# Two transformer blocks on one core: router on the unscaled activation, expert tiles in other blocks, split parts in shared places

## The chip, the cores and the metric

The kernel runs on one core of a Trainium2 chip. The metric is the device time of one execution in microseconds (us). All data is float32, and all weights come from HBM in every execution (590 MB). The engines are TensorE (PE), VectorE (DVE), ScalarE (ACT), GpSimd (POOL) and SyncE (SP), which issues most of the transfers.

## The reference, cut to what matters

There are 256 tokens of width 1024. The first block mixes (retention and attention, products with `w_in`, `w_ret_o`, `w_att_o`, `w_o`), then routes each token to 4 of 32 experts. The second block is two layers with a gated mixer or attention, a cross-attention into 256 memory rows, and feed-forward products.

```python
x = x + gt_a * (merged @ w_o)
h = rms_norm(x, g_ffn) * (1 + sc_f) + sh_f       # modulated by a vector computed from c
logits = h @ w_router + b_router                 # 256 x 32
top_val, top_idx = top_k(logits, 4); gates = softmax(top_val)
# for each expert e, over the tokens that chose it:
u = h @ w1[e] + b1[e]                            # 1024 x 2048
a = clamped_swiglu(u[:, ::2], u[:, 1::2])
x += gt_f * gate * (a @ w2[e] + b2[e])           # 1024 x 1024
```

## The kernel before

The work falls into three stages. **Stage one** (to about 350 us of the profiled span) computes the first block up to `w_o`. Its weights arrive in 1 MB tiles in six "raw" places; each half tile is split on ACT and DVE into a high and a low part (`split_now`, L196 and L197) in six places each, and PE multiplies three times (`gemm_nat`, L364). The last two such products are `wo0` and `wo1`; their epilogue (L842 to L847) updates `x`, sums its squares and writes `h2 = x * s2`, where `s2` is the scale row held in `late["ss"]`.

**Stage two** routes and runs the experts in 16 pairs, with 64 slots for each expert. The order of the jobs is `c0, c1, h0, c2, h1, ..., c15, h14, h15`: `chunk(p)` multiplies the gathered tokens of pair p by `w1` (L1028 on `bank_a`), and `second(p)` multiplies by `w2` (L1028 on `bank_b`), then scatters back (L1096) and adds to `x`. `gather(p, d)` picks the tokens by products with one-hot rows (L997); it is called for pair p + 1 while pair p is multiplied, and for pair 0 all four calls come ahead of the first product.

The expert weights come as double tiles of 2 MB ("big") in eight places, six of which lie where stage one had its raw tiles and split parts, and the first four tiles of pair 0's last step as 1 MB singles in four places of the pool `pa`: tags `x1`, `x2` (loaded first) and `reth`, `retl` (loaded last). SP issues every load in program order, and each waits until its place is free. The last twelve 1 MB tiles (the end of `h14` and all of `h15`) come in six raw places, made new where the big places were.

Before the change the router does this after `wo1`: `rsqrt` of the mean square of a token block, `h2 = h2 * rs + shift` (L897), transposes to `h2T` (L900), logits with 32 experts as rows (L909), bias on ACT (L910), a transpose back (L914), then for each block of 128 tokens the largest eight (L916), their indices, a one-hot and a count (L921); products that number the slots (L923 to L925), the gate weights, an overflow test, and the one-hot rows for pair 0 (L991).

**Stage three** is the second block, again with split weights. Ahead of it `mem_t` transposes and splits the memory rows after `h15` (L559), `mem_k(0)` multiplies them (L398 to L400), and the normed `x` is transposed (L1197) for the next product with `a_w_in` (L364).

Of the kernel before, what the change touches and what calls it, by code (L numbers as in the profile page):

```python
# [18 lines left out]
P = 128  # L19
# [77 lines left out]
class Weights:  # L97


    def __init__(self, tc, raw, nraw):  # L100
# [3 lines left out]
        self.ahead = 0  # L104
# [6 lines left out]
        self.bigs, self.doubles = None, set()  # L111
# [38 lines left out]
    def load_next(self):  # L150

        i = self.loaded
        if i in self.doubles:
# [3 lines left out]
            t = pool.tile([P, 4096], F32, name="big", tag=tag)  # L157
            v = t.rearrange("p (n k f) -> p n k f", n=2, f=ap.shape[3])
            self.history["big"].append(i)
# [10 lines left out]
    def load_free(self):  # L170

        while self.loaded < (self.limit or len(self.plan)):
            i = self.loaded
            if i not in self.early:
                h, size, n = (self.history["big"], 2, len(self.bigs)) if i in self.doubles else \
                    (self.history["raw"], 1, self.nraw)
                if len(h) >= n and h[-n] + size > self.taken:
                    break
# [11 lines left out]
    def split_now(self, i, half):  # L190
# [3 lines left out]
        hi = self.parts.tile([P, 1024], F32R, name="whi")[:, :k * f].rearrange("p (k f) -> p k f", f=f)  # L194
        lo = self.parts.tile([P, 1024], F32R, name="wlo")[:, :k * f].rearrange("p (k f) -> p k f", f=f)
# [36 lines left out]
def body(tc, A, out, offs, dbg):  # L232
# [6 lines left out]
    parts = ew.enter_context(tc.tile_pool(name="parts", bufs=6, side="right"))  # L239
# [72 lines left out]
    for kind, p_ in jobs:  # L312
        for k in range(0, 8, 2 if kind == "c" else 4):
            for e in (2 * p_, 2 * p_ + 1):
# [41 lines left out]

    def gemm_nat(key, xh, xl, w=512, kt=8, last=False):
# [5 lines left out]
        def mm(tb, xx, wpart):  # L363
            PE.matmul(pss[tb][:, :w], xx, wpart, start=n[tb] == 0, stop=n[tb] == tot - 1)  # L364
# [254 lines left out]
    def ada_late_step(j):  # L619
        if j == 4:  # L620
            late["gta"] = pt.tile([P, D], F32, name="gta")
        if j == 6:
            late["ss"] = pa.tile([P, 2, D], F32, name="ss", tag="reth")
        ada_bcast(j, gtf if j >= 10 else late["gta"] if j < 6 else late["ss"][:, j // 2 - 3])
        if j >= 8 and j < 10:
            hs = slice(j % 2 * 512, j % 2 * 512 + 512)
            g = pt.tile([P, 512], F32, name="gff", tag="aqT" if j == 8 else "akT")
# [93 lines left out]
    pt = ea.enter_context(tc.tile_pool(name="pt", bufs=1, reuse_waits="tile"))  # L721
    M = {}
# [16 lines left out]
    def att_group(g, hp):  # L739
# [6 lines left out]
        qT = pt.tile([P, 2, T], F32, name="aqT", bufs=1)  # L746
        kT = pt.tile([P, 2, T], F32, name="akT", bufs=1)
# [22 lines left out]
    def att_softmax(hp):  # L770
        for a in range(2):
# [3 lines left out]
            for g in range(3):  # L775
# [4 lines left out]
                eT = pt.tile([P, 384], F32, name="eT", bufs=2)  # L780
# [8 lines left out]
    def gate(n, h):  # L789
# [5 lines left out]
        return s_  # L795

    for st_ in stage:
# [27 lines left out]
        elif n[:2] == "wo":  # L825
            h = int(n[2])
            if h == 0:
                for k0 in range(0, 8, 2):
                    b = transpose_to(m1, "b", k0)
                    split(hh[:, k0:k0 + 2], hl[:, k0:k0 + 2], b)  # L830
                rt = pt.tile([P, 1536], F32, name="rt", tag="avt")
# [7 lines left out]
            with tc.high_priority():  # L839
                for tb in range(2):  # L840
# [3 lines left out]
                    late["sq", h] = S.activation(t, xt, AF.Square, accum_out=ss2[:, tb, h:h + 1])  # L844
                    late["h2", h] = V.tensor_tensor(h2[:, tb, hs], xt, late["ss"][:, 1, hs], OP.mult)
                    if h == 0:
                        V.tensor_scalar(ss2[:, tb, :1], ss2[:, tb, :1], 1.0 / D, RMS_EPS, OP.mult, OP.add)  # L847
    dump("x2", x)


    rt_used = [4]
# [4 lines left out]
    W.bigs = [(upper, f"big{i}") for i in range(6)]  # L856
    W.doubles = {first_b + i for i in range(0, 372, 2) if not 12 <= i < 16}
# [6 lines left out]
    def small(p, *shape):  # L864
        n = int(np.prod(shape))
        v = rt[:p, rt_used[0]:rt_used[0] + n]
        rt_used[0] += n
        if len(shape) == 2:
            v = v.rearrange("p (a b) -> p a b", a=shape[0])
        if len(shape) == 3:  # L870
# [703 lines left out]
```

## Time and profile before

| what | value |
|---|---|
| median of 3 runs | 1929.1 us (1927.86 to 1931.21) |
| the profiled execution's own time | 1928.28 us |
| its span, first to last instruction | 1926.6 us |
| PE busy | 1841.6 us (96%) |
| DVE, ACT busy | 803.5 us, 536.6 us |
| mean granted TensorE clock | 0.984 |
| read from HBM | 590.37 MB, 307 GB/s over the span |

PE is busy for most of the span in all three stages, but its busy time is modelled and does not say who waits for whom. The transfers run at 427 GB/s in most of stage two and at 145 to 300 GB/s in stage three.

### The profile page before, as it was taken

The page shows a single profiled execution, that of the slowest core. Times are in us where ns is not written, and L with a number is a line of the kernel's source. Part 1 is how long each engine was busy: PE and PEld are TensorE (multiplying, and loading weights), DVE is VectorE, ACT ScalarE, POOL GpSimd, SP SyncE. Part 2 cuts the span into 40 slices and gives each one's busy share as a digit, 9 for nine tenths or more (in the row PEclk, how much of TensorE's full clock was granted, in tenths as well). Part 3 has the DMA queues.
Part 4 walks back from the last instruction along what each step waited for, and adds up shares of the span by engine and source line. Part 5 has one row for each costly group of instructions (what it writes and reads, how often), then busy time and mean ns, then how long its engine had stood idle before and what let it go on. Part 6 is the DMA issues. An engine that isn't in the chain of part 4 may idle for free. (4 is left out here: it accounts for less than half of the span.)

```text
span 1926.6 us, 23931 instructions
## 1 busy us (share of the span) xinstructions
PE 1841.6 (96%) x10132; PEld 1212.7 (63%) x10132; DVE 803.5 (42%) x1283; ACT 536.6 (28%) x792; POOL 2.6 (0%) x7
## 2 busy tenths in 40 slices
PE   7999999899999999998999899899999999999998
PEld 6899987543344434333333344238889998879997
DVE  5787477422221212221112212028564457565445
ACT  3545454210000000000000000005544445645443
POOL 0000000000000000000000000000000000000000
PEclk9999999999999999999999999999999999999999
DMA  9777476999999999999999999998455555326550
GB/s 359 254 261 249 151 257 229 372 404 416 427 426 427 427 427 427 426 428 427 427 427 427 427 426 427 424 370 294 142 180 190 179 193 176 111 97 225 181 175 23
DMA packets 160403, 593.05 MB, mean 308 GB/s; under 512 B 7643, under 2 KB 92214, under 8 KB 134690
## 3 DMA queue, kind: packets, MB, share of 16 engines
q1 hardware_dynamic: 154008, 583.25, 77.4%
q10 hardware_dynamic: 6282, 8.21, 1.4%
q8 instruction: 81, 1.33, 0.3%
q14 instruction: 32, 0.26, 0.0%
HBM read 590.37 MB, written 1.07 MB: 307 GB/s over the span
## 5 line engine op out<-in xcount | busy, mean ns | idle before, releaser
L1028 PE MATMUL bank_a<-big,hg 128*64 128x512 f32 x2016 | 478.3, 604 | 17.0 <-DMA big<-in_w_mlp 16.9
L197 DVE TENSOR_TENSOR wlo<-raw,whi 128x1024 fp32r<-128x1024 f32 x286 | 345.4, 1222 | 252.7 <-ACT whi L196 251.7
L196 ACT ACTIVATE whi<-raw 128x1024 fp32r<-128x1024 f32 x286 | 298.2, 1058 | 346.9 <-issue 101.0
L1028 PEld LDWEIGHTS bank_a<-big,hg 128*64 128x64 f32 x2016 | 146.5, 139 | 304.1 <-issue 269.4
L1028 PE MATMUL bank_b<-big,apk 128*64 128x512 f32 x928 | 223.6, 617 | 20.7 <-DMA big<-in_w_mlp 20.7
L400 PE MATMUL bank_b<-xh,wlo 128*128 128x256 f32 x640 | 181.1, 283 | 0.0
L398 PE MATMUL bank_b<-xh,whi 128*128 128x256 f32 x640 | 181.1, 283 | 0.0
L399 PE MATMUL bank_b<-xl,whi 128*128 128x256 f32 x640 | 181.0, 283 | 0.0
L1028 PEld LDWEIGHTS bank_b<-big,apk 128*64 128x64 f32 x928 | 84.1, 141 | 148.5 <-issue 93.4
L1050 DVE COPY us<-bank_a 128x512 f32<-128x512 f32 x32 | 22.1, 692 | 345.9 <-PE bank_a L1028 345.9
L398 PEld LDWEIGHTS bank_b<-xh,whi 128*128 128x128 f32 x640 | 122.7, 192 | 0.7
L399 PEld LDWEIGHTS bank_b<-xl,whi 128*128 128x128 f32 x640 | 122.6, 192 | 0.7
L400 PEld LDWEIGHTS bank_b<-xh,wlo 128*128 128x128 f32 x640 | 122.7, 192 | 0.0
L352 ACT ACTIVATE us<-bank_a 128x512 f32<-128x512 f32 x32 | 19.1, 597 | 328.9 <-PE bank_a L1028 328.9
L1086 DVE TENSOR_TENSOR y<-bank_b,gtf 128x512 f32<-128x512 f32 x32 | 22.1, 692 | 201.6 <-PE bank_b L1028 200.1
L352 ACT ACTIVATE spread<-bank_b 128x256 f32<-128x256 f32 x16 | 6.1, 384 | 299.2 <-PE bank_b L1096 299.2
L997 PEld LDWEIGHTS bank_b<-ohg,h2c 128*128 128x128 f32 x512 | 66.1, 203 | 23.0 <-issue 21.1
L997 PE MATMUL bank_b<-ohg,h2c 128*128 128x128 f32 x512 | 72.7, 294 | 0.0
L1499 PE MATMUL bank_a<-wlo,ah 128*128 128x512 f32 x176 | 69.8, 396 | 0.0
L1500 PE MATMUL bank_a<-whi,al 128*128 128x512 f32 x176 | 69.7, 396 | 0.0
L1498 PE MATMUL bank_a<-whi,ah 128*128 128x512 f32 x176 | 69.7, 396 | 0.0
L352 ACT ACTIVATE hg<-bank_b 128x256 f32<-128x256 f32 x64 | 24.6, 384 | 149.2 <-PE bank_b L997 149.2
(382 smaller groups left out, 2735.2 us busy)
## 6 DMA issues: line engine op xcount, KB each, us to landing
big<-in_w_mlp SPq DMA_DIRECT2D x184, 2048.0 KB, 27.0
raw<-in_w_ffn_in SPq DMA_DIRECT2D x44, 1024.0 KB, 5.1
raw<-in_w_in SPq DMA_DIRECT2D x38, 1024.0 KB, 7.5
raw<-in_w_ada SPq DMA_DIRECT2D x24, 1024.0 KB, 6.6
raw<-in_w_ffn_out SPq DMA_DIRECT2D x22, 1024.0 KB, 4.9
raw<-in_w_mlp SPq DMA_DIRECT2D x16, 1024.0 KB, 14.7
raw<-in_b_w_in SPq DMA_DIRECT2D x10, 1024.0 KB, 5.2
raw<-in_w_mix_out SPq DMA_DIRECT2D x8, 1024.0 KB, 5.2
```

The lines of the kernel that those rows point to most:

```text
L196: self.nc.scalar.activation(hi, w, AF.Copy)
L197: self.nc.vector.tensor_tensor(lo, w, hi.bitcast(F32), OP.subtract)
L352: return S.activation(o, i, AF.Copy, **kw)
L398: PE.matmul(v[:, m], hi[:, k, ms], xh[:, k], start=k == 0, stop=False)
L399: PE.matmul(v[:, m], hi[:, k, ms], xl[:, k], start=False, stop=False)
L400: PE.matmul(v[:, m], lo[:, k, ms], xh[:, k], start=False, stop=k == 7)
L997: PE.matmul(b[:, n], h2c[:, tb, c0:c0 + 255:2], ohs[p_][:, tb], start=tb == 0, stop=tb == 1)
L1028: last[:] = [PE.matmul(out[at], st, w, start=start, stop=stop)]
L1050: V.tensor_copy(us[:, c + 1], u[c + 1])
L1498: PE.matmul(ops[tb, h], ah[:, k, ts], hi[:, k, hs], start=n + k == 0, stop=False)
L1499: PE.matmul(ops[tb, h], ah[:, k, ts], lo[:, k, hs], start=False, stop=False)
L1500: PE.matmul(ops[tb, h], al[:, k, ts], hi[:, k, hs], start=False, stop=n + k == 11)
```

## The change

- The router multiplies the unscaled `h2` (no `rsqrt`, no shift), with tokens as rows. The scale `rs` is applied to the logits on DVE together with a bias row `br`, to which shift times `w_router` has been added earlier (16 small transposes of the shift row to columns `shc` and 8 products, at the start of `wo0`). The transposes are placed behind the last product of `wo1`.
- `h2c` is `h2 * rs` without the shift; the shift is added when a gather leaves PSUM: on ACT for pair 0, on DVE for the others.
- The one-hot rows of pair 0 come directly behind the slot numbers; the gate weights follow, and the overflow test, the transposed gates and `spread_pair(0)` follow chunk 0.
- Of pair 0 only the first gather comes ahead of the products; the other three are called within chunk 0. The transposes of the expert bias (`b1T`) come ahead of that gather, behind the logits, and the loads of the bias rows go from SP's queue to POOL's.
- A new 16 KB place `mid` in `pa` holds the attention's small tiles, then the first double tile and every eighth later, then small tiles of stage three. It replaces the big place `middle`. The four singles now go to `reth`, `retl`, `x2`, `x1` in this order, with the first double ahead of the third; `late["ss"]` moves from `reth` to `x1`.
- A high and a low part share one of six places, taken in turn.
- The double at 370 becomes two single loads (`lone`), in the last big places; the memory rows become a planned 1 MB load ahead of `h15`'s tiles, and `mem_t` moves ahead of `h15`. The load of `g_final` goes to POOL's queue.

```diff
         pss = [bank("a") for _ in range(2)]
...
-            PE.matmul(pss[tb][:, :w], xx, wpart, start=n[tb] == 0, stop=n[tb] == tot - 1)
+            latest[:] = [PE.matmul(pss[tb][:, :w], xx, wpart, start=n[tb] == 0, stop=n[tb] == tot - 1)]
...
-        hi = self.parts.tile([P, 1024], F32R, name="whi")[:, :k * f].rearrange("p (k f) -> p k f", f=f)
-        lo = self.parts.tile([P, 1024], F32R, name="wlo")[:, :k * f].rearrange("p (k f) -> p k f", f=f)
+        both = self.parts.tile([P, 2, 1024], F32R, name="whl", tag=f"whl{(self.splits + self.shift) % 6}")
+        self.splits += 1
+        hi, lo = [both[:, n, :k * f].rearrange("p (k f) -> p k f", f=f) for n in range(2)]
...
             if h == 0:
+                for k in range(8):
+                    PE.transpose(b[:, k:k + 1], late["ss"][:1, 0, k * P:(k + 1) * P], ident[:1, :1])
+                    d0 = k // 2 * 256 + k % 2
+                    PE.transpose(b[:, 8 + k:9 + k], late["ss"][:1, 0, d0:d0 + 255:2], ident[:1, :1])
+                copy_s(shc.rearrange("p a k -> p (a k)"), b[:, :16])
+                b = bank("b")
+                for k in range(8):
+                    PE.matmul(b[:, :32], shc[:, 0, k:k + 1].to_broadcast([P, P]), wr[:, k], start=k == 0, stop=k == 7)
+                V.tensor_tensor(br, br, b[:, :32], OP.add)
...
-    W.bigs = [(upper, f"big{i}") for i in range(6)]
...
-    W.load_early(first_b + 12, pa.tile([P, 2048], F32, name="raw", tag="x1"))
-    W.load_early(first_b + 13, pa.tile([P, 2048], F32, name="raw", tag="x2"))
-    for _ in range(6):
+    W.bigs = [(pa, "mid")] + [(upper, f"big{i}") for i in range(6)]
...
+    W.lone = {first_b + 370, first_b + 371}
...
+    W.load_early(first_b + 12, pa.tile([P, 2048], F32, name="raw", tag="reth"))
+    W.load_early(first_b + 13, pa.tile([P, 2048], F32, name="raw", tag="retl"))
+    W.load_next()
+    W.load_early(first_b + 14, pa.tile([P, 2048], F32, name="raw", tag="x2"))
+    for _ in range(5):
...
-            scaled = V.scalar_tensor_tensor(h2[:, tb, hs], h2[:, tb, hs], rs, late["ss"][:, 0, hs], OP.mult, OP.add)
...
+        with after(latest[0]):
+            for tb, h in ((0, 0), (0, 1), (1, 0), (1, 1)):
+                b = bank("a" if tb > h else "b").rearrange("p (k t) -> p k t", k=4)
+                for k in range(4):
+                    PE.transpose(b[:, k], h2[:, tb, (4 * h + k) * P:(4 * h + k + 1) * P], ident)
...
+                for k in range(4 * h, 4 * h + 4):
+                    dotted = PE.matmul(lt[:, tb * 32:tb * 32 + 32], h2T[:, k, tss[tb]], wr[:, k], start=k == 0, stop=k == 7)
+        for tb in range(2):
+            if tb:
+                with after(picked):
+                    rs.append(rsqrt(ss2[:, 1, 1:], 1.0 / D, ss2[:, 1, :1], 1))
+            V.scalar_tensor_tensor(lg[:, tb], lt[:, tb * 32:tb * 32 + 32], rs[tb], br, OP.mult, OP.add)
...
+        routed = V.tensor_tensor(ohs[0], con("slots")[:, None, None, :SLOTS].to_broadcast([P, 2, 2, SLOTS]),
+                                 R[:, :, :2, None].to_broadcast([P, 2, 2, SLOTS]), OP.is_equal)
+        with after(copied):
+            for tb in range(2):
+                copy_s(h2c[:, tb], h2[:, tb], scale=rs[tb])
...
-    nc.sync.dma_start(b2, A["b_mlp2"][0])
+    nc.gpsimd.dma_start(b2, A["b_mlp2"][0])
...
-        copy_s(hg[:, p_ % 2, :, d0:d0 + 2], b.rearrange("p d e s -> p e d s"))
+        if p_ == 0:
+            for n in range(2):
+                S.activation(hg[:, 0, :, d0 + n], b[:, n], AF.Identity, bias=shc[:, 1, d0 + n:d0 + n + 1])
+            return
+        V.tensor_tensor(hg[:, p_ % 2, :, d0:d0 + 2].rearrange("p e d s -> p d e s"), b,
+                        shc[:, 1, d0:d0 + 2, None, None].to_broadcast([P, 2, 2, SLOTS]), OP.add)
...
+            if p_ == 0 and k < 6:
+                gather(0, k + 2)
...
         if (kind, p_) == ("h", 14):
             W.load_free()
-            mem_load()
-            nc.sync.dma_start(gfin, A["g_final"][None, :].to_broadcast([P, D]))
+            nc.gpsimd.dma_start(gfin, A["g_final"][None, :].to_broadcast([P, D]))
+            mem_t()
```

## Rows read from the trace of the kernel before

**Rows 1.** Busy time, clock, DMA in short stretches and in stage two.
```profile
core 0: us, PE busy (x) PEld busy (x) DVE busy (x) ACT busy (x) POOL busy (x), PEclk, DMA share, GB/s
315.00:325.00 10.00, 10.00 (x44) 7.94 (x43) 5.01 (x5) 4.87 (x6) 0.00 (x0) 1.00 0.02 7
325.00:330.00 5.00, 4.18 (x27) 3.40 (x26) 4.99 (x8) 2.22 (x4) 0.00 (x0) 1.00 0.68 223
365.00:370.00 5.00, 5.00 (x29) 4.88 (x28) 0.00 (x0) 1.16 (x3) 0.00 (x0) 0.58 1.02 434
410.00:420.00 10.00, 10.00 (x51) 4.44 (x51) 2.51 (x6) 0.77 (x2) 0.00 (x0) 1.00 0.85 329
480.00:1150.00 670.00, 635.03 (x2890) 258.41 (x2888) 136.79 (x242) 48.94 (x93) 0.00 (x0) 0.98 1.01 427
...
1282.00:1286.00 4.00, 4.00 (x18) 1.29 (x16) 0.00 (x0) 0.00 (x0) 0.00 (x0) 0.75 0.54 197
```

**Rows 2.** Issues on SP in order of time: start, length, what, how many.
```profile
306.35 19.32 SPq L133 DMA_DIRECT2D raw<-in_w_mlp  x2
...
390.82 0.80 SPq L133 DMA_DIRECT2D big<-in_w_mlp  x2
...
414.20 1.17 SPq L133 DMA_DIRECT2D big<-in_w_mlp  x2
```

**Rows 3.** What SP waited for, 250 to 480 us: total, times, longest.
```profile
SPq L133 <- PE bank_a L1028: 81.9, 9, 22.5
```

**Rows 4.** Instructions in order of time, end of `wo1` to first expert product.
```profile
349.60 0.39 PE L364 MATMUL bank_a<-whi,hl 128*128 128x512 f32 x1
...
352.69 0.21 DVE L431 TENSOR_SCALAR rs_z<-rt 128x1 f32<-128x1 f32 x1
...
354.09 1.41 DVE L897 SCALAR_TENSOR_TENSOR h<-h,rs_y,ss 128x512 f32<-128x512 f32 x2
...
359.52 0.20 DVE L916 MAX8 rt<-bank_b 128x8 f32<-128x32 f32 x1 [0.51 <-PE bank_b L914]
...
360.60 0.37 DVE L921 TENSOR_REDUCE rt<-rt 128x32 f32<-128x128 f32 x1
...
363.44 6.60 PE L997 MATMUL bank_b<-ohg,h2c 128*128 128x128 f32 x32
...
369.97 7.52 PE L1028 MATMUL bank_a<-big,hg 128*64 128x512 f32 x34
```

**Rows 5.** PE in order of time, between chunk 0 and chunk 1.
```profile
397.59 1.09 PE L1008 MATMUL bank_b<-cm,b 64*128 64x64 f32 x8
...
398.89 3.93 PE L997 MATMUL bank_b<-ohg,h2c 128*128 128x128 f32 x32
```

**Rows 6.** Groups by line and shape, 284 to 371 us: busy us, mean ns.
```profile
L909 PE MATMUL bank_b<-h2T,rt 128*32 128x128 f32 x32 | 4.1, 275 | 0.2 <-ACT h2T L352 0.2
...
L559 PE MATMUL bank_b<-cm,m 128*128 128x128 f32 x16 | 2.2, 272 | 0.0
```

**Rows 7.** DVE in order of time: last use of the `g_ffn` row.
```profile
316.88 0.69 DVE L630 SCALAR_TENSOR_TENSOR ss<-ss,gff 128x512 f32<-128x512 f32 x1 [0.99 <-ACT ss L352]
```

**Rows 8.** PE in order of time, start of `h15`.
```profile
1276.15 1.07 PE L1028 MATMUL bank_b<-raw,apk 128*64 128x512 f32 x2
...
1280.34 8.78 PE L1028 MATMUL bank_b<-raw,apk 128*64 128x512 f32 x32 [3.12 <-DMA raw<-in_w_mlp]
```

**Rows 9.** PE in order of time, end of stage two to first product of stage three.
```profile
1301.23 1.38 PE L559 MATMUL bank_b<-cm,mem 128*128 128x128 f32 x8
...
1303.74 0.39 PE L399 MATMUL bank_a<-mem_l,whi 128*128 128x256 f32 x1
...
1309.97 1.04 PE L1197 MATMUL bank_b<-cm,x 128*128 128x128 f32 x8
...
1312.07 0.50 PE L364 MATMUL bank_a<-whi,xh 128*128 128x512 f32 x1 [1.06 <-ACT xh L352]
```

**Rows 10.** DMA issues: queue, count, KB each, median us from issue to landing.
```profile
b<-in_b_mlp SPq DMA_DIRECT2D x3, 128.0 KB, 25.6
...
rt<-in_w_router ACTq DMA_DIRECT2D x1, 128.0 KB, 8.0
```

More of the change, by code (lines that the diff above doesn't have):

```diff
@@ L103, in __init__ @@
         self.loaded = self.done = self.taken = 0
-        self.ahead = 0
+        self.ahead = self.splits = self.shift = 0
         self.parts = None
@@ L110, in __init__ @@
         self.limit = None
-        self.bigs, self.doubles = None, set()
+        self.bigs, self.doubles, self.lone = None, set(), set()
         self.history = {"raw": [], "big": []}
@@ L152, in load_next @@
         i = self.loaded
-        if i in self.doubles:
+        if i in self.doubles or i in self.lone:
             ap = self.plan[i][1]
@@ L174, in load_free @@
             if i not in self.early:
[L175 to L177 removed]
+                h, n = (self.history["big"], len(self.bigs)) if i in self.doubles | self.lone else \
+                    (self.history["raw"], self.nraw)
+                if len(h) >= n and h[-n] + (2 if h[-n] in self.doubles else 1) > self.taken:
                     break
@@ L622, in ada_late_step @@
         if j == 6:
-            late["ss"] = pa.tile([P, 2, D], F32, name="ss", tag="reth")
+            late["ss"] = pa.tile([P, 2, D], F32, name="ss", tag="x1")
         ada_bcast(j, gtf if j >= 10 else late["gta"] if j < 6 else late["ss"][:, j // 2 - 3])
@@ L626, in ada_late_step @@
             hs = slice(j % 2 * 512, j % 2 * 512 + 512)
-            g = pt.tile([P, 512], F32, name="gff", tag="aqT" if j == 8 else "akT")
+            g = mid[:, (j - 8) * 512:(j - 7) * 512]
             nc.scalar.dma_start(g, A["g_ffn"][:, hs].to_broadcast([P, 512]))
@@ L721, in body @@
     pt = ea.enter_context(tc.tile_pool(name="pt", bufs=1, reuse_waits="tile"))
+    mid = pa.tile([P, 4096], F32, name="mid", tag="mid")
+    eTs = [mid[:, 1024 + i * 384:1024 + (i + 1) * 384] for i in range(2)]
     M = {}
@@ L883, in body @@
     ixf = small(P, 2, 8)
+    lg = small(P, 2, 32)
     oh = small(P, 2, 4, 32)
     pick = small(P, 2, 32)
+    ohs = {0: keep.tile([P, 2, 2, SLOTS], F32, name="ohg0", tag="GT")}
     ones = con("ones")
[L887 to L910 removed]
@@ new lines, in body @@
+    gates = small(P, 2, 4)
+    with after(routed):
+        V.tensor_tensor(gates, mx[:, :, :4], mx[:, :, :1].to_broadcast([P, 2, 4]), OP.subtract)
+        S.activation(gates, gates, AF.Exp)
+        gl = small(P, 2)
+        V.reduce_sum(gl, gates, AX.X)
+        V.reciprocal(gl, gl)
+        V.tensor_tensor(gates, gates, gl[:, :, None].to_broadcast([P, 2, 4]), OP.mult)
+        for tb in range(2):
+            V.tensor_tensor(oh[:, tb], oh[:, tb], gates[:, tb, :, None].to_broadcast([P, 4, 32]), OP.mult)
+            V.reduce_sum(G[:, tb], oh[:, tb].rearrange("p k e -> p e k"), AX.X)
@@ L1200, in transposed @@
         return v_, s_
-    mem_t()
     kmT, vm = [], []
-    kv = kv_[0]
+    mid = pa.tile([P, 4096], F32, name="kv", tag="mid")
+    kv = mid[:, :2048].rearrange("p (n i b t) -> p n i b t", n=2, i=2, b=2)
     for n, to in enumerate((kmT, vm)):
@@ L1266, in body @@
         nc.gpsimd.memset(q, 0.0)
[L1268 removed]
+    junk = mid[:, 3584:].bitcast(mybir.dt.bfloat16)
     def normalize(dst, src, st, n, gb):
```

214 lines of the change are left out of this document (96 added, 118 removed).

## The prediction

> **What bounds the kernel now.** I read the short stretches first. In stage two the DMA engines are full at 427 GB/s from 480 to 1150 us [rows 1], and PE, 635 of 670 us busy, waits for tiles now and then: that stage lasts as long as its stream of expert tiles. So the question is when the stream gets going and when it ends.
>
> Two holes stand ahead of it. From 315 to 325 us the queues carry 7 GB/s [rows 1]: SP issued a first single tile at 306.35 us, and the second waits in front of everything else until `x2` is free, 19 us later [rows 2]. The other is at 410 to 420 us, with the DMA share at 0.85 [rows 1]. There the list of issues has nothing between 390.82 and 414.20 us [rows 2], and the wait view gives the reason: 22.5 us for PE in chunk 1 [rows 3]. The eight doubles and four singles are full, and the next places come free only when PE has finished the first step of chunk 1. PE has worked without a wait for data since its first expert product at 369.97 us [rows 4]. So the start of the endless part of the stream hangs on PE, and PE's start on the router: 19.97 us from the last product of `wo1` (350.0) to 369.97 [rows 4]. Filling the first hole alone only makes the second longer.
>
> The end: `h15` waits 3.12 us for a tile, and its first 32 instructions then take 8.78 us [rows 8]. Behind it PE does the memory transposes (1301.23), a dense `mem_k(0)` until 1309.97, the transposes of `x`, and the first product at 1312.07 [rows 9]. Stage three is mostly PE-bound, so what is won before 1312 should stay won.
>
> **The change part by part: the router.** L is the end of the last `wo1` product (350.0 before).
> - PE: 16 transposes at 2.2/16 = 0.14 us and 32 logit instructions at 4.1/32 = 0.13 us [rows 6], 6.3 us; the second block's logits are done at L + 6.3, the first block's about L + 4.3. The new logits load 128 columns and stream 32 instead of the reverse; I take them as equal.
> - DVE: bias and scale (estimate 0.25 us, as the 0.21 of a small operation [rows 4]) and the picking chain, 359.52 to 360.97 = 1.45 us [rows 4], for block one end at L + 6.0. The second `rsqrt` is ordered behind it: 352.69 to 354.09 = 1.4 us [rows 4]. The second chain ends at L + 9.1. The scaling of `h2` (1.41 us [rows 4]), the bias and the transpose back are gone; `h2c` on ACT runs beside this.
> - From the end of the picking to the first gather lie 363.44 − 360.97 = 2.5 us [rows 4], of which I take about 1.0 for gate weights and overflow, now later: L + 10.6.
> - The first gather is a quarter of 3.93 us at full clock [rows 5], 1.0, and its two evacuations 0.4: L + 12.0.
> - The other three gathers are only moved: 2.95 us of PE inside chunk 0. The bias transposes (1.09 us [rows 5]) leave it for a time when PE waits anyway. Net, PE stands where it stood at 369.97 at L + 13.9: 6.1 us won.
> - Against it, 16 one-row transposes and 8 products (two instructions each) enter `wo0`, where PE has no slack but 0.82 us in 325 to 330 [rows 1]. 32 instructions at 0.105 to 0.15 us (my estimate around the 0.13 above) are 3.4 to 4.8, less 0.8: I take 2.6. Bounds 0 (they fit into waits earlier) and 4.0.
> - The clock: in 365 to 370 us it was granted at 0.58 on average, after a thin stretch of PE work, and the 32 gather instructions took 6.60 us instead of 3.93 [rows 1, 4, 5]. Now the first products may meet it. The old number contains 2.7 us of it; I charge 1.3 to the new, between 0 and 2.7, because PE is idle for some 4 us, where it was thinly used from 350 to 363.
>
> The Trainium skill (TensorE: Matmul & The Clock Gate, "What's actually happening") says that the slow clock is the default and sustained activity lifts it. By that the new start pays the 2.7 in full, and the forecast below would be 1.4 us later. The rows agree with the rule in kind.
>
> So the router gives 6.1 − 2.6 − 1.3 = 2.2 us; ends −0.6 and 6.1.
>
> **Loads.** Two singles and the first double can now go while `x2` is still read: `reth` and `retl` are free, and `mid` at 316.88 + 0.69 = 317.57 us [rows 7]. That puts one more single and the double, 3.15 MB, at 427 GB/s 7.4 us, into the first hole. By the paragraph above this is worth nothing by itself; it caps the gain at the front at about 7.4 us, above the 2.2. Its cover is the full set of places at 390 us. Parts that come free in turn let doubles issue a few us earlier; same answer. The bias rows on POOL's queue are priced under the rivals.
>
> **Hidden edits.** Adding the shift on DVE costs at most some 0.7 us for each of 60 gathers (the 512-wide `L630` took 0.69 [rows 7]); DVE is busy 137 of 670 us [rows 1], and the gathers run a pair ahead: nothing, or 2.8 us a pair if PE ever waited for the bank. `lone`, `mid` in stage three and shared places move no bytes.
>
> **The end.** `mem_t` ahead of `h15` falls into the 3.12 us wait [rows 8]. If PE works there, the first 32 instructions take 32 × 7.52/34 = 7.1 us [rows 4] rather than 8.78, and the last tiles, whose places they free, are issued so much earlier; the queue is half empty there (0.54 [rows 1]). I take 1.3 us, bounds 0 and 1.7. The memory tile takes a raw place and so lets one expert tile fewer be ahead, but before, the same bytes stood in the same queue: nothing, at worst one tile, 1.05 MB or 2.45 us. Behind `h15`, transposes and their first wait vanish: `mem_k(0)` runs dense from 1303.74 to 1309.97 [rows 9], 6.2 us, and could start at about 1301.3, where the transposes start now. So it ends at 1307.5: I take 2.5 us, bounds 0 (another load is late then) and 3.6 (the norm of `x` is last then; my estimate of its DVE chain).
>
> **Sum.** 2.2 + 1.3 + 2.5 = 6.0 us off the profiled execution's 1928.28 (its span is 1926.6) gives 1922.3. That execution lies 0.8 under the median of 1929.1, so I forecast 1923.1 for the median. About 0.2% (3.9 us) is what a measurement of this kernel can tell from no change.
>
> **Rivals.**
> - *The stream moves by the full 7.4 us.* If the extra work in `wo0` hides and the clock stays up, PE wins 6.1 or more and the earlier loads are used: 7.4 + 3.8 = 11.2, 1917.9. For it: the hole is real [rows 1]. Against it: PE was full around `wo0`.
> - *The router's gain is eaten.* Both charges at their upper ends: 6.1 − 4.0 − 2.7 = −0.6, leaving 3.8 − 0.6 = 3.2: 1925.9. For it: 10.00 of 10 us of PE in 315 to 325 [rows 1].
> - *The memory transposes do not move.* The order on each engine is set by the builder's own timeline, and `h15` is marked urgent; if PE gets the transposes behind it as before, only 2.2 remain: 1926.9.
> - *Slower: the first gather waits for the bias rows.* The transposes of the bias rows stand ahead of it on PE, and everything behind waits with them. On SP's queue the rows landed 25.6 us after issue, a small load on ACT's queue 8.0 us [rows 10]. If their place (tag `y`) comes free only with the router's tiles, as at L + 10 before, 25.6 us would push the gather some 25 us back: 22 lost at the front, 3.8 won at the end, 1947. At 8.0 us it costs about as much as is won. It decides from a landing later than about L + 20. Against it: the place lies over small tiles of the modulation, whose last use is near 317 us [rows 7], so the loads can go in the empty hole. The Trainium skill (DMA: Bandwidth & Descriptors, "Issuing engines are not separate DMA queues") says that loads from any engine share the same DMA engines and interleave, so that POOL's queue would not by itself bring the rows sooner; the 8.0 beside 25.6 us says that standing behind 2 MB tiles in one queue does matter here.
>
> **How the numbers follow.** Forecast 0.46, full 7.4 us 0.13, eaten gain 0.22, transposes that stay 0.09, late bias rows 0.10. Faster by over 0.2%: 0.46 + 0.13 = 0.59; within: 0.22 + 0.09 = 0.31; slower: 0.10. The likeliest case alone spans 1919 to 1925. The range takes in the second to fourth cases with some slack and leaves the late rows out: 1915.5 to 1930.
>
> **What would show it.** Right: `wo1` ends some 2.6 us later, the first expert product comes at L + 12 to L + 14, the issue at 414.20 moves to about 412, and the empty stretch ahead of it grows by some 5 us; the hole at 315 shrinks; memory transposes near 1274, `h15` without a half-clock start, first product of stage three near 1306. Wrong: no empty stretch at 400 to 412 us (then the loads counted), `wo1` ending later than 354, a PE wait for the bias rows, or a time lost in stage three, where a load of parameters that used to be in time is now late.

## The result and the profile after

The changed kernel took 1938.73 us (median of 7 runs, 1935.62 to 1941.83) beside 1927.86 for the kernel before (7 runs, 1925.51 to 1931.21): a ratio of 1.0055, 95% interval 1.0043 to 1.0067. It is slower by some 10.9 us, outside the stated range of 1915.5 to 1930 and on the other side of the forecast of 1923.1. The profiled execution took 1938.29 us, with a span of 1936.6 against 1926.6.

Four points, each the start of an instruction, cut both spans into five stretches, so the differences add up to the span's, but for rounding.

| stretch, us | before | after | predicted | found |
|---|---|---|---|---|
| to the last product of `wo1` | 349.60 | 358.62 | +2.6 | +9.0 |
| from there to the first issue behind the empty stretch of SP | 64.60 | 62.86 | -4.8 | -1.7 |
| from there to the last product of `h15` | 882.9 | 882.5 | -1.3 | -0.4 |
| from there to the first product of stage three | 14.96 | 15.35 | -2.5 | +0.4 |
| from there to the end | 614.5 | 617.3 | 0 | +2.8 |
| sum | | | -6.0 | +10.0 |

The last product of `h15` starts at (before, then after):

```profile
1297.11 0.59 PE L1028 MATMUL bank_b<-raw,apk 128*64 128x512 f32 x1
...
1303.94 0.59 PE L1058 MATMUL bank_b<-raw,apk 128*64 128x512 f32 x1
```

Short stretches of the changed kernel, as [rows 1] of before: times, busy time and number of instructions by engine, granted clock, DMA share, GB/s.

```profile
315.00:325.00 10.00, 10.00 (x41) 7.40 (x41) 6.52 (x8) 4.99 (x6) 1.59 (x3) 1.00 1.04 360
365.00:370.00 5.00, 1.28 (x7) 1.06 (x6) 4.20 (x22) 1.15 (x1) 0.00 (x0) 0.69 1.00 415
370.00:375.00 5.00, 4.94 (x25) 4.76 (x26) 4.07 (x21) 1.43 (x4) 0.00 (x0) 0.50 1.02 434
380.00:385.00 5.00, 5.00 (x25) 1.56 (x22) 0.00 (x0) 0.00 (x0) 0.00 (x0) 1.00 0.01 3
410.00:420.00 10.00, 9.30 (x51) 3.78 (x49) 6.13 (x10) 3.69 (x5) 0.00 (x0) 1.00 0.63 264
480.00:1150.00 670.00, 635.39 (x2914) 255.88 (x2914) 156.62 (x295) 31.63 (x48) 0.00 (x0) 0.99 1.01 427
```

The hole at 315 is filled (360 GB/s instead of 7), and in exchange the queues run dry at 380 to 385 us and more than before at 410 to 420 (share 0.63 instead of 0.85). Between 480 and 1150 nothing differs. The issues behind still wait for PE, up to 18.2 us at a time, so the early loads seem worth nothing, as predicted; no run took them out alone. What SP waited for between 250 and 480 us, and the issues around the empty stretch (start, length, what):

```profile
SPq L133 <- PE bank_a L1058: 86.6, 10, 18.2
...
402.47 0.80 SPq L133 DMA_DIRECT2D big<-in_w_mlp  x2
...
421.48 0.80 SPq L133 DMA_DIRECT2D big<-in_w_mlp  x2
```

The gap that ended at 414.20 [rows 2] ends at 421.48. It did not grow by some 5 us, as the prediction's sign had it: from start to start it is 19.0 us instead of 23.4. It is the queues that stand empty for longer. The router on PE, as [rows 4]:

```profile
358.62 0.40 PE L373 MATMUL bank_a<-whl,hl 128*128 128x512 f32 x1
358.85 0.60 PE L926 MATMUL bank_b<-cm,h 128*128 128x128 f32 x4
...
362.38 2.87 PE L934 MATMUL bank_b<-rt,h2T 128*128 128x32 f32 x24 [0.25 <-ACT h2T L359]
...
371.69 6.24 PE L1023 MATMUL bank_b<-ohg,h2c 128*128 128x128 f32 x30
377.87 7.09 PE L1058 MATMUL bank_a<-big,hg 128*64 128x512 f32 x32
```

L, the end of the last `wo1` product, is 359.0. The first gather comes at L + 12.7 (before 363.44 - 350.0 = 13.4), and 30 gather instructions stand ahead of the first product at L + 18.9, not 8. On DVE, the first block's bias, the second's, and the one-hot rows:

```profile
365.28 0.25 DVE L939 SCALAR_TENSOR_TENSOR rt<-bank_b,rs_y,rt 128x32 f32<-128x32 f32 x1 [2.23 <-PE bank_b L934]
...
368.29 0.25 DVE L939 SCALAR_TENSOR_TENSOR rt<-bank_b,rs_y,rt 128x32 f32<-128x32 f32 x1
...
370.99 0.42 DVE L951 TENSOR_TENSOR ohg<-cm,R 128x256 f32<-128x256 f32 x1
```

The first block's chain waited for the logits of both blocks (L + 6.3, not L + 4.3). Ahead of `wo0`, the new instructions and the products before them on PE:

```profile
325.20 5.79 PE L373 MATMUL bank_a<-whl,att 128*128 128x512 f32 x24
330.91 0.22 PE L859 MATMUL bank_b<-cm,ss 1*128 1x1 f32 x1
...
332.78 1.97 PE L865 MATMUL bank_b<-rt,shc 128*128 128x32 f32 x16 [0.27 <-ACT shc L359]
334.59 1.94 PE L568 MATMUL bank_b<-cm,m 128*128 128x128 f32 x16
```

The shift row takes PE from 330.91 to 334.59, 3.7 us. The first row holds the surprise: 24 products in 5.79 us. The kernel before does the same 24 (first and last shown) in this time:

```profile
319.69 0.39 PE L364 MATMUL bank_a<-whi,att 128*128 128x512 f32 x1
...
324.91 0.39 PE L364 MATMUL bank_a<-whi,att 128*128 128x512 f32 x1
```

From first start to last start, 23 steps, that is 5.22 us, 0.227 a product; after, (5.79 - 0.39)/23 = 0.235. No wait stands in either. The median over all 128x512 products of stage one at the full clock went from 0.227 to 0.234, 3% more. The end of stage two on PE, as [rows 8] and [rows 9]:

```profile
1283.59 1.91 PE L568 MATMUL bank_b<-cm,raw 128*128 128x128 f32 x16
1285.61 7.94 PE L1058 MATMUL bank_b<-raw,apk 128*64 128x512 f32 x34
1296.63 3.65 PE L1058 MATMUL bank_b<-raw,apk 128*64 128x512 f32 x16 [3.09 <-DMA raw<-in_w_mlp]
...
1314.06 0.29 PE L409 MATMUL bank_a<-mem_h,whl 128*128 128x256 f32 x1
1314.19 1.03 PE L1228 MATMUL bank_b<-cm,x 128*128 128x128 f32 x8
1319.29 1.22 PE L373 MATMUL bank_a<-whl,xh 128*128 128x512 f32 x2 [4.07 <-ACT xh L359]
```

The memory transposes moved as meant, and `h15` runs at the full clock behind them (granted 1.00 at 1282 to 1286 us, 7.94 us for 34 instructions). But PE reaches the end of what has landed and waits 3.09 us there, and 0.60 more at 1300.89, where before it waited 3.12 us [rows 8] and

```profile
1290.35 7.35 PE L1028 MATMUL bank_b<-raw,apk 128*64 128x512 f32 x30 [1.23 <-DMA raw<-in_w_mlp]
```

So the transposes did not fill the wait: it stands further on, and the end of `h15` still follows its last tiles. The memory products behind it run dense, but PE then waits 4.07 us for ACT. What ACT and its queue (ACTq) did:

```profile
1312.42 0.39 ACTq L1280 DMA_DIRECT2D ws<-in_a_w_s  x1
1312.85 2.62 ACTq L1282 DMA_DIRECT2D tri<-in_c_tri  x1
1315.51 0.71 ACTq L1284 DMA_DIRECT2D bsr<-in_a_b_s  x1
1316.27 1.06 ACT L201 ACTIVATE whl<-raw 128x1024 fp32r<-128x1024 f32 x1 [2.92 <-issue]
1317.23 0.58 ACT L359 ACTIVATE kv<-bank_a 128x512 f32<-128x512 f32 x1
1317.71 1.05 ACT L201 ACTIVATE whl<-raw 128x1024 fp32r<-128x1024 f32 x1
1318.65 1.08 ACT L359 ACTIVATE xh<-bank_b 128x512 fp32r<-128x512 f32 x2
```

ACT spent 3.7 us on issuing three loads of tables, then did a split, the copy of `kv` and a second split before the copy that PE waited for.

### The profile page after: what moved, and what is told of

It is laid out like the page before. It is cut to its first block, busy times and chain, and to the rows that moved or that the text cites. A ratio compares the mean times of both kernels' runs of the same rounds, so it can differ in the third digit from the quotient of the medians.

```text
span 1936.6 us, 23949 instructions
## 1 busy us (share of the span) xinstructions
PE 1843.4 (95%) x10162; PEld 1210.6 (63%) x10162; DVE 825.7 (43%) x1342; ACT 514.7 (27%) x735; POOL 4.7 (0%) x11
## 5 line engine op out<-in xcount | busy, mean ns | idle before, releaser
L202 DVE TENSOR_TENSOR whl<-raw,whl 128x1024 fp32r<-128x1024 f32 x286 | 345.6, 1222 | 260.1 <-ACT whl L201 258.7
L201 ACT ACTIVATE whl<-raw 128x1024 fp32r<-128x1024 f32 x286 | 298.6, 1058 | 333.0 <-issue 109.8
L409 PE MATMUL bank_b<-xh,whl 128*128 128x256 f32 x640 | 180.9, 283 | 0.0
L408 PE MATMUL bank_b<-xl,whl 128*128 128x256 f32 x640 | 180.3, 282 | 0.0
L407 PE MATMUL bank_b<-xh,whl 128*128 128x256 f32 x640 | 180.1, 281 | 0.0
L407 PEld LDWEIGHTS bank_b<-xh,whl 128*128 128x128 f32 x640 | 120.9, 189 | 0.6
L408 PEld LDWEIGHTS bank_b<-xl,whl 128*128 128x128 f32 x640 | 120.6, 189 | 0.7
L409 PEld LDWEIGHTS bank_b<-xh,whl 128*128 128x128 f32 x640 | 119.9, 187 | 0.0
L373 PE MATMUL bank_a<-whl,hh 128*128 128x512 f32 x288 | 91.2, 399 | 0.0
L1028 DVE TENSOR_TENSOR hg<-bank_b,shc 128x256 f32<-128x256 f32 x60 | 25.4, 424 | 123.9 <-PE bank_b L1023 123.9
L1531 PE MATMUL bank_a<-whl,al 128*128 128x512 f32 x176 | 69.2, 393 | 0.0
L1529 PE MATMUL bank_a<-whl,ah 128*128 128x512 f32 x176 | 68.8, 391 | 0.0
```

The costliest lines, as they stand in the source:

```text
L201: self.nc.scalar.activation(hi, w, AF.Copy)
L202: self.nc.vector.tensor_tensor(lo, w, hi.bitcast(F32), OP.subtract)
L373: latest[:] = [PE.matmul(pss[tb][:, :w], xx, wpart, start=n[tb] == 0, stop=n[tb] == tot - 1)]
L407: PE.matmul(v[:, m], hi[:, k, ms], xh[:, k], start=k == 0, stop=False)
L408: PE.matmul(v[:, m], hi[:, k, ms], xl[:, k], start=False, stop=False)
L409: PE.matmul(v[:, m], lo[:, k, ms], xh[:, k], start=False, stop=k == 7)
```

## The experiments

The kernel before was run beside each group. Its median was 1927.01 with the first four, then 1928.47, 1927.29 and 1928.25, so ratios are compared, not times; 0.0010 of a ratio is 1.9 us. By their intervals, the difference of two runs' ratios is uncertain by 3 to 4 us, so what a single edit is worth is read from the traces where they can tell.

**Where the operands lie.** `shc` (64 bytes a partition) and `nov` (32) are new in the pool `keep`, and everything in `pa` behind it moved by 96 bytes: `hh` from byte 34272 to 34368 of each partition. In the feed-forward part of stage three `ah` moved from 90688 to 105120. The split weights `whi`, `wlo` or `whl` start 480 past a multiple of 512 in both kernels. (The addresses are those the program assigns when it is built; no trace shows them.)

```diff
 # e1_pad: the changed kernel, plus
+    keep.tile([P, 8], F32, name="pad")
 # e2_pad_both: as e1_pad, plus
+        pf.tile([P, 8], F32, name="pad2")
 # e3_before_pad: the kernel before, plus
+    keep.tile([P, 24], F32, name="pad")
 # e8_shift_right: the changed kernel, plus
+    ew.enter_context(tc.tile_pool(name="pad_r", bufs=1, side="right")).tile([P, 8], F32, name="padr")
```

> The changed kernel with 32 unused bytes in the pool ahead of the activations, so that hh, hl, reth and att lie 32 bytes past a multiple of 64 in each partition, as they did before the change; ah and al then lie on a multiple of 64, as before. Theory places (stage one is longer because its 128x512 products start 234 ns apart instead of 227, and that follows from where the activations lie): the spacing in stage one returns to 227 ns, some 600 products give back 4.0 us, those of stage three's other products 0.8, while the 528 products of the feed-forward part go from 229 to 234 ns and lose 1.9: 2.9 us less, 1935.8. Rival order (the shared places mid and whl changed who waits for whom, and the spacing is a by-product of waits): spacing still 234 in stage one, time within 1 us of 1938.7.

> As the run before, and 32 unused bytes more ahead of ah and al, so that they too lie 32 past a multiple of 64. Theory places: 227 ns in stage one and 227 to 230 in the feed-forward part: 4.8 us less than the changed kernel, 1933.9. Rival order: within 1 us of 1938.7.

> The kernel before with 96 unused bytes in the same pool and nothing else: hh on a multiple of 64, ah 32 past one, exactly where the changed kernel has them. Theory places: stage one loses 4.0 us at 234 ns a product, the last product of wo1 ends near 354, other products of stage three lose 0.8, the feed-forward part gains 1.9: 2.9 us more than before, 1930.8. Rival order: spacing stays 227, time within 1 us of 1927.9.

> The changed kernel with 32 unused bytes at the other end, so that in stage one the split weights whl lie on a multiple of 64 as hh does (stage three's are not moved). Which operand sets the pace: if it is where the activations lie, nothing changes (234 ns, 1938.7); if it is that both lie alike, stage one returns to 227 ns and gains 4.0, 1934.7; if the weights must lie 32 past a multiple of 64, stage one gets slower still. Rival order: 234 ns, within 1 us of 1938.7.

Measured: e1_pad 1938.42, ratio 1.0056 (1.0042 to 1.0070); e2_pad_both 1935.49, 1.0049 (1.0035 to 1.0063); e3_before_pad 1930.14, 1.0014 (1.0005 to 1.0023); e8_shift_right 1936.56, 1.0048 (1.0034 to 1.0062). The same 24 products in e3_before_pad, first and last of them on PE:

```profile
324.71 0.40 PE L365 MATMUL bank_a<-whi,att 128*128 128x512 f32 x1
...
330.10 0.39 PE L365 MATMUL bank_a<-whi,att 128*128 128x512 f32 x1
```

5.39 us instead of 5.22: 96 unused bytes alone turn 0.227 into 0.234, in a kernel with no other edit. The rival (order and shared places) falls. My rule of where hh lies falls too: e1_pad puts it back 32 past a multiple of 64, and the group becomes 5.73 us, 0.232, not 0.227. e8_shift_right moves the other operand and gives the same 5.73, on PE in e1_pad and in e8_shift_right:

```profile
321.79 5.73 PE L374 MATMUL bank_a<-whl,att 128*128 128x512 f32 x24
```

```profile
322.34 5.73 PE L374 MATMUL bank_a<-whl,att 128*128 128x512 f32 x24
```

What these two have in common is the distance from the activations to the split weights, 384 modulo 512. In e2_pad_both (1935.49 instead of the expected 1933.9) stage one has the 0.232 of e1_pad, not 0.227, and the feed-forward part, at distance 256, has 0.227. So the theory became one of distance:

```diff
 # e9_place: the changed kernel, plus
+    keep.tile([P, 40], F32, name="pad")
+        pf.tile([P, 40], F32, name="pad2")
 # e10_before_place: the kernel before, plus
+        pf.tile([P, 104], F32, name="pad2")
```

> The changed kernel with 160 unused bytes ahead of the activations and 160 more ahead of ah and al. After the first runs the theory is narrower: what sets the spacing of 128x512 products is the distance from the left operand's address to the split weights' address, taken modulo 512 bytes. Seen so far: 0 gives 227 ns, 256 gives 228, 288 gives 234, 320 gives 229, 384 gives 232 to 235, 416 gives 234 to 236. Here it is 256 in stage one and 0 in the feed-forward part. Theory distance: 227 to 229 ns in both, the end of wo1 some 4 to 5.5 us earlier, the feed-forward part 1.3 shorter, other products of stage three 0.8: 6 to 7 us less than the changed kernel, 1932.2. Rival (the shared places whl themselves cost, not the distance): stage one stays at 232 or more, at most 2 us won, 1936.7.

> The kernel before with 416 unused bytes ahead of ah and al alone, which brings their distance to the split weights from 416 to 0 modulo 512. Theory distance: the 528 products of the feed-forward part go from 234 to 227 ns, 4.0 us less than before, 1923.0; stage one and two unchanged. Rival: the feed-forward part waits for its weights and not for the products: within 1 us of 1927.0.

Measured: e9_place 1935.33, 1.0039 (1.0024 to 1.0054); e10_before_place 1925.27, 0.9985 (0.9977 to 0.9994). The group in e9_place:

```profile
320.15 5.60 PE L374 MATMUL bank_a<-whl,att 128*128 128x512 f32 x24
```

That is 0.227 again, at distance 256. In the feed-forward part PE starts 707 instead of 700 instructions in 1450 to 1550 us in e10_before_place. The kernel before carried this cost itself, and repairing that alone makes it faster by 0.15%, 2.9 of the 4.0 us expected. In e9_place 3.1 us of the 6 to 7 expected came; the intervals exclude neither 6 nor nothing. The traces can tell: e11_combo (below), which has the places of e9_place, and e5_two_banks have the same code and the same slow stretch up to there, and the last `wo1` product starts at 354.77 and 358.92 us, 4.2 us apart. The rival of the shared places falls, since stage one is at 0.227 with them in use.

**The thin work ahead of wo0.** The new instructions left out:

```diff
 # e4_no_rows: the changed kernel; the 16 transposes, copy_s(shc, ...), 8 products and br + ... replaced by
+                V.tensor_copy(shc.rearrange("p a k -> p (a k)"), late["ss"][:, 0, :16])
```

> The changed kernel without the 16 transposes of the shift row and the 8 products with it ahead of wo0; shc is filled by one copy of other numbers on DVE, so the bias of the logits and the shift of the gathered rows are left out of the computation in effect. Theory thin work: PE saves 3.7 us (330.91 to 334.59 in the profile after), and also the stretch at the lower clock level that begins near 328 to 332 us in five of eight profiles with these instructions and in none without them, 3.4 to 6.8 us long, at half speed up to 3.4 us: 3.7 to 6 us less, about 1934. The prediction's price: 2.6 us less, 1936.1. Rival (wo0's first products wait for their split weights anyway): within 1 us of 1938.7.

Measured: 1933.78, 1.0033 (1.0020 to 1.0045), about 4.2 us less than the changed kernel, nearer to the theory than to 2.6, though the intervals don't part the two. In the traces of e16_gathers_behind, which has these instructions, and e4_no_rows, neither with a slow stretch near 50 or 330 us, the last `wo1` product starts at 355.83 and 352.47: the instructions alone cost 3.4 us. Of the 12 profiles taken of kernels with these instructions, 9 have a stretch at the lower clock level that begins at 326 to 333 us, though the changed kernel's own has none; of the 5 taken without the one-row transposes (before, e3_before_pad, e10_before_place, e4_no_rows, e12_combo_dma) none has. (The expectation's "five of eight" should read five of seven.) Windows of e5_two_banks, columns as above:

```profile
325.00:330.00 5.00, 4.73 (x31) 3.77 (x29) 3.85 (x7) 2.30 (x3) 0.00 (x0) 1.00 0.60 203
330.00:335.00 5.00, 5.00 (x25) 5.00 (x25) 1.48 (x3) 0.60 (x1) 0.00 (x0) 0.50 0.97 342
```

The granted clock is 0.50, 1.2 GHz, right behind the one-row transposes. Its price: in the profile of e14_no_lone, which has it, the last product of `wo1` is

```profile
361.81 0.40 PE L373 MATMUL bank_a<-whl,hl 128*128 128x512 f32 x1
```

and in that of the changed kernel it starts at 358.62, with the same code up to there and the same earlier stretch near 50 us: 3.2 us.

**The router.**

```diff
 # e5_two_banks: the changed kernel
-        lt = bank("b")
+        lts = [bank("b"), bank("b")]
 # e16_gathers_behind: the changed kernel; in chunk 0, behind the products of each step
+            if p_ == 0:
+                with after(*last):
+                    if k < 6:
+                        gather(0, k + 2)
+                    gather(1, k)
```

> The changed kernel with the logits of the two token blocks in two banks of PSUM instead of one, so that the first block's bias need not wait for the second block's 16 products. Theory router chain: the first picking chain starts at L + 4.3 instead of L + 6.4 (L: the end of the last wo1 product), everything behind comes 2 us earlier, the first expert product at L + 17, the first issue of the endless stream 2 us earlier: 1936.7. Rival (the chain is not what the start waits for, as the first products still stand behind three gathers at the slow clock): the first product comes earlier but the issue does not, 1938.7.

> The changed kernel with the later gathers of pair 0 and all of pair 1's ordered behind the products of each step of chunk 0, as the change's description has it; in the changed kernel PE got 30 gather instructions ahead of the first product. The prediction's step (the gathers are only moved, PE has to do them ahead of the first release either way): the first product comes at L + 15.5 instead of L + 19.2, but the first release of the endless stream only as much earlier as fewer gathers fall into the slow stretch, 0 to 1.5 us: 1938. Rival (products at once help): 3.7 us less, 1935.

Measured: e5_two_banks 1936.28, 1.0042 (1.0027 to 1.0057); e16_gathers_behind 1938.49, 1.0052 (1.0039 to 1.0066). In e5_two_banks L is 359.3, and on DVE the first bias starts at

```profile
364.12 0.25 DVE L939 SCALAR_TENSOR_TENSOR rt<-bank_b,rs_y,rt 128x32 f32<-128x32 f32 x1
```

L + 4.8 instead of L + 6.3. The first gather then starts at L + 11.3 instead of 12.7, in all three runs with two banks. On SP the issue behind the empty stretch is

```profile
419.63 0.33 SPq L133 DMA_DIRECT2D big<-in_w_mlp  x1
```

at L + 60.3 instead of 62.5, the 2 us that were expected. In e7_tables, with one bank and L at 360.9, it is

```profile
422.06 0.33 SPq L133 DMA_DIRECT2D big<-in_w_mlp  x1
```

So not all of the 2 us is the bank's. The stretch at the lower clock level behind L lasts 6.8 us in e5_two_banks and 10.2 in the changed kernel, and three runs with one bank and a stretch of 6.8 us (e4_no_rows, e6_mem_behind, e7_tables) have the issue at L + 61.1 to 61.3. So some 1 us is shown for the second bank, and 1.2 us goes with the shorter stretch; whether that one follows from the bank is open. In the three runs with two banks it lasts 6.8 us; of the eleven with one bank three have 6.8, seven 10.2 and one 13.7. In e16_gathers_behind L is 356.2, and PE shows

```profile
368.91 2.07 PE L1023 MATMUL bank_b<-ohg,h2c 128*128 128x128 f32 x8
371.50 8.54 PE L1058 MATMUL bank_a<-big,hg 128*64 128x512 f32 x32 [0.52 <-ACT hg L1026]
```

The first product is at L + 15.3, 3.6 us earlier, and the issue at L + 62.4, where it was, with a slow stretch of the same 10.2 us. So it is the work that counts ahead of the first release; which gather comes first is worth nothing.

**The end of stage two and the start of stage three.**

```diff
 # e7_tables: the changed kernel
-    nc.scalar.dma_start(ws, ...), (tri, ...), (bsr, ...)
+    nc.gpsimd.dma_start(ws, ...), (tri, ...), (bsr, ...)
 # e6_mem_behind: the changed kernel, mem_load and mem_t as before
-                W.add(("mem", 0), kpf(A["mem_2"][0], 0, D, 0, 2), True)
 # e14_no_lone: the changed kernel; e15_mem_no_lone: e6_mem_behind, both with
-    W.lone = {first_b + 370, first_b + 371}
```

> The changed kernel with three loads of small tables at the start of stage three issued from POOL instead of ACT (ws, tri, bsr). Theory tail: ahead of the first product of stage three PE waits 4.07 us for ACT's copy of xh, because ACT spends 2.62 and 0.71 us on issuing two of these loads and has two splits and the copy of kv behind them; without them the first product comes 3 us earlier, the stretch of slow clock behind the wait (1319 to 1323) goes or gets shorter, worth up to 1.7 more: 3 to 4.7 us less, 1934.9. Rival (the norm of x is last anyway, so the copy of xh comes no earlier): within 1 us of 1938.7. Rival two: the slow issue moves to POOL and the tables are late for their transposes: no gain, or a later wait.

> The changed kernel with the memory rows loaded and transposed as before the change: a load of their own from SP's queue, transposes behind h15. The prediction's step: the move is worth 1.3 us within h15 and 2.5 us behind it, so 3.8 us more, 1942.5. Theory tail: the first product of stage three waits for the copy of xh on ACT and not for the memory products, so behind h15 nothing is lost; at most the 1.3 us: within 1.5 us of 1938.7.

> The changed kernel with its last two expert tiles ahead of the raw places loaded as one double again, as before the change. Theory pay-back (the change lost some 3.5 us at the end of stage two by loading the last double as two singles, and the planned memory load only won that back): 3 us less or so, 1935.5, and less waiting in h15. Rival (the single loads cost nothing; the move of the memory work itself is worth 4): within 1 us of 1938.7.

> The run with the memory rows as before the change (1942.9), and the last double loaded as one as well, so that the end of stage two is fed as before. Theory pay-back: from the first release to the end of h15 882.9 us as before, against 886.4 in that run, 1939.3. Rival: still 886, 1942.9.

Measured: e7_tables 1934.28, 1.0031 (1.0022 to 1.0040), 4.6 us less. PE in e7_tables:

```profile
1315.12 1.03 PE L1228 MATMUL bank_b<-cm,x 128*128 128x128 f32 x8
1317.40 0.73 PE L373 MATMUL bank_a<-whl,xh 128*128 128x512 f32 x2 [1.25 <-ACT xh L359]
```

The wait of 4.07 is 1.25, and the stretch from the last product of `h15` is 12.09 us instead of 15.35: 3.3 us that the trace shows. Issued from POOL the three loads took 1.06, 0.55 and 0.53 us of a queue that nothing waits for.

e6_mem_behind took 1942.88, 1.0070 (1.0055 to 1.0085), some 3 us more than the changed kernel. e14_no_lone took 1940.12, 1.0060 (1.0047 to 1.0073), and e15_mem_no_lone, with the memory rows as before, 1942.19, 1.0073 (1.0060 to 1.0086), 2.5 us more than that. Both pairs lie between the prediction's price of 3.8 and my theory of at most 1.5, and their intervals do not part the two. Loading the last double whole won nothing in either pair, where 3 us or so were expected: the single loads cost nothing that shows, and the pay-back theory falls.

**The repairs together.** The DMA version brings the shift to its columns through HBM:

```diff
 # e11_combo: e9_place + e5_two_banks + e7_tables; e12_combo_dma: e11_combo, transposes and their copy replaced by
+                sd = scratch.tile([1, D], F32, name="shd")
+                nc.gpsimd.dma_start(sd, late["ss"][:1, 0])
+                nc.gpsimd.dma_start(shc[:, 0], sd.rearrange("o (k p) -> p (o k)", p=P))
+                nc.gpsimd.dma_start(shc[:, 1].rearrange("p (a n) -> p a n", n=2),
+                                    sd.rearrange("o (a p n) -> p (o a) n", p=P, n=2))
```

> The changed kernel with three repairs together: places as in the run with 160 unused bytes twice, logits in two banks, tables from POOL. Measured one at a time they moved the ratio to before from 1.0055 to 1.0039, 1.0042 and 1.0031: 3.1, 2.5 and 4.6 us. If they add up: 10.2 us less, 1928.5, the same as before. If the stretches at the lower clock level hide or eat a part: 1930 to 1932.

> As the run before, and the shift reaches its columns by three small transfers from POOL's queue through a scratch row in HBM instead of the 16 transposes; the 8 products stay. Theory thin work: 1.9 us of PE go (16 transposes and the wait for their copy), and the slow stretch at 328 to 332 us comes less often, up to 2 us more: 2 to 4 us less than the run before, 1925.5. Rival: the transfers of 4 bytes a piece land late and the 8 products wait for them: no gain, or a PE wait ahead of wo0.

Measured: e11_combo 1928.45, 1.0003 (0.9994 to 1.0012); e12_combo_dma 1925.20, 0.9982 (0.9972 to 0.9993). The three repairs add up to the 10 us, and the fourth gives 4 more. The changed kernel so repaired is 0.18% faster than the kernel before, as much as the kernel before gains from better places alone (e10_before_place). So with the found costs repaired the change is still worth nothing; the stretches of the two profiles show where its gains go:

| stretch, us | e10_before_place | e12_combo_dma | difference |
|---|---|---|---|
| to the last product of `wo1` | 351.09 | 351.64 | +0.6 |
| to the first issue behind the empty stretch | 64.57 | 60.33 | -4.2 |
| to the last product of `h15` | 881.87 | 883.70 | +1.8 |
| to the first product of stage three | 14.76 | 12.09 | -2.7 |
| to the end | 611.89 | 615.77 | +3.9 |

Most of the router's 4.8 and the tail's 2.5 are there, and are given back behind. In the expert stage the same stretch took 881.9 us in e11_combo, so the 1.8 are no firm number; but e9_place, e11_combo and e12_combo_dma, whose feed-forward products have the distance of e10_before_place, all take 615.4 to 615.8 us for the last stretch. The 8 products follow the 24 directly (PE in e12_combo_dma):

```profile
326.48 1.87 PE L865 MATMUL bank_b<-rt,shc 128*128 128x32 f32 x16
```

## Why the prediction was wrong

- **"Enter `wo0`, where PE has no slack: 2.6 us"** was mis-sized and, above all, taken for the whole cost of stage one. Found +9.0 in the profiled pair: 4.3 from places (e3_before_pad minus e10_before_place at the last `wo1` product, 355.41 - 351.09, with the same slow stretch at 50 us), 3.2 left for the thin work (the changed kernel minus e3_before_pad, 358.62 - 355.41, the same slow stretch again), and 1.5, put down to a slow stretch near 50 us that is longer in this execution (6.8 us instead of 3.4) and that the kernel before can have too (e10_before_place, with 6.8, against before, 351.09 - 349.60, the same code up to there). The step that failed was unspoken: that code which is not edited keeps its pace, a term put at nothing that measured 4.3 us. The prediction's sign of being wrong, `wo1` ending later than 354, came at 359.0. The 2.6 stood at the low end of its own sum (3.4 to 4.8, less 0.8). The part's upper bound of 4.0 held for the instructions, but not for the slow clock behind them, another 3.2 us in most profiles, though not in the changed kernel's own. I had charged the clock only behind the router.
- **"The first block's logits are done about L + 4.3, the chains end L + 6.0 and 9.1"**: right for the products, wrong for the wait. Both blocks shared a bank, and the first chain waited for the last product; shown by e5_two_banks, 1.4 us at the first gather and about 1 at the issue where the slow stretch is the same.
- **"First gather L + 12.0 done, three inside chunk 0"**: the builder put more gathers ahead of the first product, at the slow clock, which spoils the predicted L + 12 to 14; but that the other gathers are only moved was right, and e16_gathers_behind shows that the order is worth nothing. In all the router won 1.7 of 4.8 us in the changed kernel's profile, and 3.5 to 4.3 in the three with two banks (60.3 to 61.1 us instead of 64.6).
- **"The clock: I charge 1.3, between 0 and 2.7"**: too little, though inside its bounds. 30 gather instructions took 6.24 us, beside 6.60 for 32 before, and at the pace of the full clock [rows 5] they would take 3.7: 2.6 us, not 1.3. The granted clock is 0.50 at 370 to 375 us. The Trainium skill (TensorE: Matmul & The Clock Gate, "What's actually happening"), by which the new start would pay in full, agrees with these rows.
- **Loads worth nothing, stream unchanged, bias rows in time, shift on DVE hidden**: right as far as the traces show. The rival of late bias rows did not happen: their loads were issued by 318.59 us and landed in 7.4 us (median), long before their transposes at 370.62. That the time came out slower, as in that rival, has other reasons.
- **"`mem_t` ahead of `h15` falls into the 3.12 us wait"**, taken at 1.3 us: the half-clock start went as forecast, but PE then waits 3.09 us further on, and the stretch to the end of `h15` is only 0.4 us shorter.
- **"`mem_k(0)` ends at 1307.5: I take 2.5"**: the move was right, the cover was gone. What is late next was named as the norm of `x`, at no cost to the 2.5; it was ACT. Its issues of tables ran before in the shade of `mem_k(0)` and now stood in front of the copy of `xh`. Without them 14.96 - 12.09 = 2.9 us are won against before, as forecast, but not kept: behind the first product PE waits again, 0.64 us for the norm (`rs_y`) and 0.37 for a split in e12_combo_dma, and from the last product of `h15` to the end that run takes 627.9 us, e10_before_place 626.7.
- **"What is won before 1312 should stay won"**: 2.8 us more went in stage three. Starts of equal instructions, compared one by one, lie 7.2 us later at the first product and 9.4 by 1325 us, where slow clock and late splits meet; 1.5 more go by 1400 and 1.4 near 1700; the two feed-forward parts give back 1.3 and 1.1 by their better distance. The 1.5 by 1400 contain a stretch of 3.4 us at the lower clock level, from 1394; 7 of the 14 profiles of the changed kernel and its variants have one between 1380 and 1405, none of the 3 of the kernel before. In e12_combo_dma stage three still takes 3.9 us more behind its first product than in e10_before_place. Which of the edits causes that stays open, and so does why taking the memory move back costs some 3 us, when in the profiled pair the move won 0.4 us within `h15` and lost 0.4 behind it.

The Trainium skill (SBUF — State Buffer, "Operand start alignment") says that an operand must start at a multiple of its element's size, and that this is about legality and not speed. All starts here obey it; the spacing still differs between 0.227 and 0.235 us, so that rule does not answer the question of speed.

## What to carry to other kernels

A new small tile in a pool moves every tile behind it. Compare the spacing of untouched products before and after, and, where it differs, the distance of the two operands modulo 512, before looking for a cause among the edits. When work is moved out of a stretch, list what the other engines did in its shade, their DMA issues too: it becomes the wait. A few tiny instructions on a busy PE cost their time and, often, a stretch at half the clock behind them (here in 9 of 12 profiles). And compare a repaired kernel with a kernel before that has the same repair: here nothing was left of the forecast 6.0 us.

## What the runs showed of the hardware that was not expected

The median spacing of 128x512 products (moving operand `whl` or `whi` and `wlo`, the other `hh`, `hl`, `att`, `ah` or `al`) at full clock depends on the difference of the two start addresses (weights minus the other) modulo 512 bytes: 0 gave 227 ns (before in stage one, e10_before_place in the feed-forward part), 256 gave 227 (e9_place in stage one, e2_pad_both in the feed-forward part), 288 gave 234 (e1_pad, feed-forward), 320 gave 229 (after and e3_before_pad, feed-forward), 384 gave 232 (e1_pad and e8_shift_right), 416 gave 234 (after in stage one, before in the feed-forward part). A period of 256 fits these six as well as one of 512. The products of 256 columns changed their pattern (120 each, or 116 and 125 in turn) but not their mean. What in the chip makes the distance matter was not tried.
